# Keeping an intermediate weight combination in SBUF between the two products of a Winograd-Strassen unit that need it

## Chip, cores and metric

The kernel runs on one core of a Trainium2 chip. The metric is the device time in microseconds (us). The engines are TensorE (PE; PEld is its weight load), VectorE (DVE), ScalarE (ACT), GpSimd (POOL) and SyncE (SP), which issues the DMAs of this kernel. Each engine takes its instructions in the order in which they were written down for it, and waits on semaphores for what the others make.

## Reference

One decoder layer over 2048 positions of width 1024, in float32. An input projection is cut into two head groups, a gated MLP (A) and a Mamba-2 scan (B); their outputs are joined and projected back.

```python
h = rms_norm(x, pre_w)
proj = jnp.einsum('bld,dc->blc', h, w_in)
u, v, zg, z, xbc, dt_raw = jnp.split(proj, SPLITS, axis=-1)
y_a = spatial_gating(u, v, zg, v_norm_w, v_norm_b, ws, bs, gmlp_norm_w)
y_b = ssd_mixer(xbc, z, dt_raw, conv_w, conv_b, dt_bias, a_log, d_skip, ssd_norm_w)
mixed = jnp.einsum('blc,cd->bld', jnp.concatenate([y_a, y_b], axis=-1), w_out)
return x + rms_norm(mixed, post_w)
```

## The kernel before

The two projections are cut into seven **units**, numbered 0 to 6 (the list `UNITS`). Each unit multiplies a 2x2 arrangement of blocks of the activations (side A) with a 2x2 arrangement of blocks of the weights (side B), by the seven products P1 to P7 of the Winograd form of Strassen's scheme. Units 0 to 5 go through the sets (P1, P2), (P6, P7), (P4), (P5, P3); within a set through two block pairs p, the products, and two halves j. This makes 28 **steps** a unit, in each of which PE runs 24 matmuls of 128x512: every float32 operand is split into a high and a low part, and `mm3` (L165 to L167) forms three partial products. Unit 6 is the output projection, with four halves j and 56 steps.

Side B of a step is made by `make_b`, once for both pairs p. It loads blocks of 128x1024 (512 KB) into tiles "r" of `rpool` (7 buffers), combines them on DVE, and `split` writes the high part (ACT, L160) and the low part (DVE, L161) to a tile "b" of `bpool` (5 buffers). With q, t, r the blocks (0,1), (1,1), (0,0) of the weights, P6 forms T3 = t - q (L795) and **T2 = T3 + r** (L800). T2 is multiplied in P6, and is needed again in P4, whose operand is block (1,0) minus T2 (L819). P7 takes T3 from its tile; P5 subtracts two loaded blocks (L815). Between P6 and P4, T2 goes to DRAM and back: `store` puts the write on a list (L801), from which SP issues it some 5 us of the program's own count later (L230), and P4 loads it as a second tile "r" (L817, issued at L153). Side A of units 1 to 5 needs no arithmetic: it is loaded ready split, 1 MB a step (L736), into 3 buffers. In unit 0, S2, the like intermediate of side A, is already kept in SBUF by two POOL copies (L749) and two subtractions of halves (L773).

Beside the products run **tasks**: generators that are advanced between steps and put the scan of group B (lines 359 to 475) and the gating of group A (lines 553 to 627) between the matmuls. The names that matter here: `E` is a decay matrix, loaded from DRAM (L381), shifted (L389), passed through the exponential (L394) and masked (L431); `xdt` (L434) and E feed the matmuls `y_ps` (L448); `junk` (L184) is the output of a sum of squares, whose result goes through `s_ms`/`g_ms` (L171, DVE) and `s_r`/`g_r` (L173, POOL) to the scaling of `y` (L471, L627, both ACT). L598 and L613 on DVE and L615 on ACT belong to the gating.

`after` (L868) takes the accumulators `acc` away. P1 is copied out by ACT (L876), and P2 is then summed onto the same accumulator: its first matmul on each of the four accumulators waits for the copy of P1. `acc` has 5 banks of PSUM. SBUF tiles of 128x512 come from `gpool` (32 buffers), for the tasks, the stores and the copies of S2.

The order on each engine is set ahead of the run by the Tile scheduler, by its own reckoning of when data and buffers come free. A removed or added instruction can thus change the order of others.

Of the kernel before, what the change touches and what calls it, by code (L numbers as in the profile page):

```python
# [11 lines left out]
ALU = mybir.AluOpType  # L12
# [39 lines left out]
def hybrid_kernel(ctx: ExitStack, tc: tile.TileContext, x, x_t, pre_w, w_u, w_o, w_dt,  # L52
                  v_w, v_b, ws_t, bs_t, gn_w, conv_w, conv_b, dt_bias, a_log, d_skip, sn_w,
                  post_w, out):
    nc = tc.nc
# [15 lines left out]
    def gfull(name):  # L71
        return gpool.tile([P, 3 + T], F32, name=name, tag="g")

    def gt(name):
        return gfull(name)[:, 0:T]
# [4 lines left out]
    def rt(name):  # L80
        return rpool.tile([P, 2, T], F32, name=name, tag="r")
# [8 lines left out]
    t_d = {(u, j): dram.tile([P, 2, T], F32, name=f"t{u}{j}") for u in range(7) for j in range(2 if u < 6 else 4)}  # L90
# [58 lines left out]
    def load(pieces):  # L149
        res = []  # L150
        for src in pieces:
            t = rt("r")
            nc.sync.dma_start(out=t, in_=src)  # L153
            res.append(t)
        return res

    def split(pool, name, t):

        w = pool.tile([P, 2, 2, T], F32R, name=name)
        nc.scalar.activation(w[:, :, 0, :], t, AF.Copy)  # L160
        nc.vector.tensor_tensor(w[:, :, 1, :], t, w[:, :, 0, :], ALU.subtract)  # L161
        return w
# [61 lines left out]
    def store(dst, src, then=None):  # L224
        stores.append((now[0] + BEHIND, dst, src, then))
# [554 lines left out]
            store(a_d[p][name, j], w[:, :, :, :].bitcast(F32))  # L780
        yield w

    t3 = {}

    def make_b(u, name, j):
        piece = lambda k, n: w_u[u, k, n, j] if u < 6 else w_o[k, n, j]
        tt = nc.vector.tensor_tensor
        if name in PLAIN_B:
            t, = load([piece(*PLAIN_B[name])])
            yield  # L790
        elif name == "P6":
            if u < 6:
                q, t, r = load([piece(0, 1), piece(1, 1), piece(0, 0)])
                yield
                tt(t, t, q, ALU.subtract)  # L795
                t3[u, j] = t
            else:
                t, r = load([t3_d[j], piece(0, 0)])
                yield
            tt(r, t, r, ALU.add)  # L800
            store(t_d[u, j], r)  # L801
            t = r
        elif name == "P7":
            if u < 6:
                yield
                t = t3.pop((u, j))
            else:
                t, q = load([piece(1, 1), piece(0, 1)])
                yield
                tt(t, t, q, ALU.subtract)  # L810
                store(t3_d[j], t)
        elif name == "P5":
            t, q = load([piece(0, 1), piece(0, 0)])
            yield
            tt(t, t, q, ALU.subtract)  # L815
        else:
            t, q = load([piece(1, 0), t_d[u, j]])  # L817
            yield
            tt(t, t, q, ALU.subtract)  # L819
        yield split(bpool, "b", t)  # L820
# [12 lines left out]
    def look_ahead(i):  # L833
# [10 lines left out]
        def load_b(n, u, p, name, j):  # L844
            if p == 0:
                made_b[u, name, j] = make_b(u, name, j)
                next(made_b[u, name, j])
# [74 lines left out]
    for group in groups:  # L922
        i = group[0]
        u, p, name, j = steps[i][:4]
        _, channels, _, nj = UNITS[u]
# [81 lines left out]
```

## Time and profile before

| | |
|---|---|
| Runs | 1585.33, 1588.78, 1590.7 us; median 1588.78 us |
| Profiled execution | own time 1584.35 us, span 1582.6 us |
| Mean granted TensorE clock | 0.979 |
| Busy share | PE 95%, PEld 80%, DVE 68%, ACT 52%, POOL 25% |
| DMA | 494.63 MB, mean 313 GB/s |

The span runs from the first to the last instruction of the profiled execution; its own time holds 1.75 us more. A busy share is the part of the span in which an engine worked. A wait is idle time of an engine just before an instruction, put down to what ended it. Unit 1 begins at about 244 us, unit 2 at 439, unit 3 at 632, unit 4 at 829, unit 5 at 1032 and unit 6 at 1254 us.

### The profile page before, as it was taken

What the parts mean: (1) busy time and instruction counts of PE and PEld (TensorE: products, weight loads), DVE (VectorE), ACT (ScalarE), POOL (GpSimd) and SP (SyncE); (2) the same over time, 40 slices, a digit from 0 to 9 for tenths busy, and PEclk for the clock granted to TensorE, in tenths of its full rate; (3) what the DMA queues carried; (4) which work ended last, traced back from release to release, by engine and by line L of the source; (5) the groups of instructions that cost most, each with busy time, mean ns of one, the idle gap of its engine ahead of it and who ended that gap; (6) DMA issues with size and microseconds to landing.
All of it is one profiled execution on the core that took longest, in us unless ns stands there. A gap on an engine that the chain in (4) does not pass through costs nothing.

```text
span 1582.6 us, 21521 instructions
## 1 busy us (share of the span) xinstructions
PE 1508.9 (95%) x7268; PEld 1258.4 (80%) x7268; DVE 1068.9 (68%) x1708; ACT 819.8 (52%) x1769; POOL 390.1 (25%) x449
## 2 busy tenths in 40 slices
PE   4979999899999999999999999989999999999996
PEld 3868887788888888888778888867888878888775
DVE  3476874678665576567786768764665646587698
ACT  4432324655676545654466666859737742333332
POOL 1000000234232333342234515353523300000022
PEclk9988999999999999999999999989999999999999
DMA  9799999999998799986998788866776598897998
GB/s 333 264 371 357 338 411 397 392 340 366 374 349 311 240 353 341 329 316 238 333 338 319 271 299 275 279 229 225 276 252 242 193 302 326 275 384 239 341 351 333
DMA packets 160847, 494.63 MB, mean 313 GB/s; under 512 B 19040, under 2 KB 35808, under 8 KB 140768
## 3 DMA queue, kind: packets, MB, share of 16 engines
q1 hardware_dynamic: 160736, 493.25, 85.9%
q8 instruction: 57, 0.93, 0.2%
q14 instruction: 54, 0.44, 0.1%
HBM read 373.51 MB, written 119.67 MB: 312 GB/s over the span
## 4 chain that ended last, share of the span: by engine, by line
PE 57%; DMA 13%; DVE 11%; ACT 7%; issue 3%; POOL 1%; SPq 1%; DVEq 0%; ACTq 0%; POOLq 0%
PE acc L165 16%; PE acc L167 16%; PE acc L166 16%; DMA E<-scr 3%; DMA r<-yd 3%; PE y_ps L448 3%; ACT E L389 2%; DMA r<-w_o 2%; PE y_ps L451 1%; PE st_ps L453 1%; DVE cv_out L372 1%; DVE a L161 1%; PE s_ps L594 1%; PE y_tp L553 1%; DVE b L161 1%
## 5 line engine op out<-in xcount | busy, mean ns | idle before, releaser
L165 PE MATMUL acc<-b,a 128*128 128x512 f32 x1344 | 544.6, 406 | 16.1 <-DMA a<-as0P 5.4
L166 PE MATMUL acc<-b,a 128*128 128x512 f32 x1344 | 527.3, 392 | 0.0
L167 PE MATMUL acc<-b,a 128*128 128x512 f32 x1344 | 520.2, 393 | 4.3 <-DVE a L161 4.3
L165 PEld LDWEIGHTS acc<-b,a 128*128 128x128 f32 x1344 | 253.7, 189 | 71.3 <-DMA a<-as0P 5.6
L167 PEld LDWEIGHTS acc<-b,a 128*128 128x128 f32 x1344 | 253.2, 188 | 60.2 <-DVE a L161 6.3
L166 PEld LDWEIGHTS acc<-b,a 128*128 128x128 f32 x1344 | 254.0, 189 | 49.3
L160 ACT ACTIVATE a<-r 128x1024 fp32r<-128x1024 f32 x96 | 101.1, 1057 | 200.8 <-PE acc L167 88.5
L165 PE MATMUL acc<-a,b 128*128 128x512 f32 x448 | 182.4, 414 | 8.3 <-ACT b L160 4.2
L372 DVE SCALAR_TENSOR_TENSOR cv_out<-cv_raw,cw,cv_out 128x512 f32<-128x512 f32 x192 | 155.1, 810 | 41.5 <-ACT cv_out L370 39.5
L161 DVE TENSOR_TENSOR b<-r,b 128x1024 fp32r<-128x1024 f32 x112 | 141.9, 1270 | 60.6 <-ACT b L160 60.4
L166 PE MATMUL acc<-a,b 128*128 128x512 f32 x448 | 180.3, 403 | 0.8 <-DVE a L161 0.8
L167 PE MATMUL acc<-a,b 128*128 128x512 f32 x448 | 177.7, 400 | 0.0
L160 ACT ACTIVATE b<-r 128x1024 fp32r<-128x1024 f32 x112 | 117.2, 1052 | 86.9 <-PE acc L167 33.1
L161 DVE TENSOR_TENSOR a<-r,a 128x1024 fp32r<-128x1024 f32 x96 | 117.3, 1223 | 50.5 <-ACT a L160 50.3
L165 PEld LDWEIGHTS acc<-a,b 128*128 128x128 f32 x448 | 87.2, 195 | 27.4 <-ACT b L160 4.3
L184 ACT ACTIVATE junk<-y 128x128 bf16<-128x128 f32 (+1 forms) x192 | 65.5, 341 | 83.1 <-POOL y L465 71.4
L457 POOL TENSOR_TENSOR state<-state,ex 128x256 f32<-128x256 f32 x60 | 46.9, 781 | 239.5 <-PE y_ps L451 239.4
L166 PEld LDWEIGHTS acc<-a,b 128*128 128x128 f32 x448 | 86.8, 194 | 19.6 <-DVE a L161 1.8
L167 PEld LDWEIGHTS acc<-a,b 128*128 128x128 f32 x448 | 86.4, 193 | 18.9 <-issue 0.2
L436 POOL TENSOR_TENSOR xde<-xtok,dte 128x256 f32<-128x256 f32 x64 | 52.3, 824 | 165.0 <-ACT xtok L408 158.7
L173 POOL TENSOR_TENSOR o_r<-o_ms,mhalf 128x1 f32<-128x1 f32 x16 | 19.0, 1198 | 295.1 <-DVE o_ms L171 285.0
L389 ACT ACTIVATE E<-E,cs 128x128 f32<-128x128 f32 x256 | 79.6, 390 | 22.2 <-DMA E<-scr 22.2
(163 smaller groups left out, 2125.8 us busy)
## 6 DMA issues: line engine op xcount, KB each, us to landing
a<-as0P SPq DMA_DIRECT2D x64, 1024.0 KB, 7.4
a<-as1P SPq DMA_DIRECT2D x64, 1024.0 KB, 6.2
r<-w_u SPq DMA_DIRECT2D x108, 512.0 KB, 6.4
r<-yd SPq DMA_DIRECT2D x72, 512.0 KB, 5.3
r<-hd SPq DMA_DIRECT2D x48, 512.0 KB, 7.5
r<-w_o SPq DMA_DIRECT2D x36, 512.0 KB, 5.2
E<-scr SPq DMA_DIRECT2D x64, 256.0 KB, 7.4
yd<-yT SPq DMA_DIRECT2D x64, 256.0 KB, 4.4
```

Source lines behind the costliest of these rows:

```text
L160: nc.scalar.activation(w[:, :, 0, :], t, AF.Copy)
L161: nc.vector.tensor_tensor(w[:, :, 1, :], t, w[:, :, 0, :], ALU.subtract)
L165: nc.tensor.matmul(dst, lhsT=a_hi, rhs=b_hi, start=first, stop=False, skip_group_check=True)
L166: nc.tensor.matmul(dst, lhsT=a_hi, rhs=b_lo, start=False, stop=False, skip_group_check=True)
L167: return nc.tensor.matmul(dst, lhsT=a_lo, rhs=b_hi, start=False, stop=last, skip_group_check=True)
L173: nc.gpsimd.tensor_tensor(r, ms, mhalf[:, 0:n], ALU.pow)
L184: nc.scalar.activation(junk[:, 0:n], src, AF.Square, accum_out=dst)
L372: nc.vector.scalar_tensor_tensor(cv, raw[:, j:j + T], cw[:, ti, j:j + 1], cv, ALU.mult, ALU.add)
L389: nc.scalar.activation(E[:, h, :], E[:, h, :], AF.Relu, scale=-1.0, bias=dts[self.b]["cs"][:, o + h:o + h + 1])
L436: nc.gpsimd.tensor_tensor(h4(xde[:, :]), xc, hv(d["dte"], g, c), ALU.mult)
L448: nc.tensor.matmul(yps[:, h * HD:(h + 1) * HD], lhsT=E[:, h, :], rhs=xdt[:, h * HD:(h + 1) * HD], start=True, stop=True)
L457: nc.gpsimd.tensor_tensor(h4(st[:, :]), h4(st[:, :]), ev(d["ex"], 1, g, c), ALU.mult)
```

## The change

In units 1 to 5, T2 is no longer written to DRAM. Two POOL copies put its halves in two tiles `t2` of `gpool`, and P4 loads block (1,0) alone and subtracts the halves one by one on DVE. Units 0 and 6 stay as they were.

```diff
-    t3 = {}
+    t3, t2_in = {}, {}
...
             tt(r, t, r, ALU.add)
-            store(t_d[u, j], r)
+            if 0 < u < 6:
+                t2_in[u, j] = [gt("t2") for _ in range(2)]
+                for kk in range(2):
+                    nc.gpsimd.tensor_copy(t2_in[u, j][kk], r[:, kk, :])
+            else:
+                store(t_d[u, j], r)
             t = r
...
+        elif 0 < u < 6:
+            t, = load([piece(1, 0)])
+            yield
+            for kk, t2 in enumerate(t2_in.pop((u, j))):
+                tt(t[:, kk, :], t[:, kk, :], t2, ALU.subtract)
         else:
             t, q = load([piece(1, 0), t_d[u, j]])
```

Lines behind the change move: L876 is L886 in the changed kernel, L901 is L911, the copies stand at L804, the subtraction of P5 at L820 and that of the halves at L825.

**ACT, unit 4, second pair, around P1.** Before, from the gating's `sg` up to the scaling by `g_r`. In these rows `p1` is the copy of P1.

```order
L394 ACT_TABLE_LOAD
...
L160 ACTIVATE b_7770<-r_7692 128x2x512 [waits PE_49]
...
L876 ACTIVATE p1_7700<-acc_7618 128x512 [waits DMAHW7_49,PE_49]
L876 ACTIVATE p1_7708<-acc_7633 128x512 [waits PE_49]
...
L184 ACTIVATE junk_253,g_ss_7533<-y_7503 128x128 [waits Activation_49,Pool_49]
L876 ACTIVATE p1_7723<-acc_7640 128x512 [waits PE_49]
...
L184 ACTIVATE junk_253,g_ss_7533<-y_7503 128x128 [waits Activation_49]
L471 ACTIVATE y_7314<-y_7314,s_r_7604 128x256 [waits Pool_49]
...
L876 ACTIVATE p1_7754<-acc_7662 128x512 [waits PE_49]
...
L627 ACTIVATE y_7455<-y_7455,g_r_7671 128x128 [waits Pool_49]
```

The same stretch of the changed kernel; the four loads of ACT's tables ahead of it are the first rows.

```order
L394 ACT_TABLE_LOAD
...
L615 ACT_TABLE_LOAD
...
L394 ACT_TABLE_LOAD
...
L615 ACT_TABLE_LOAD
...
L184 ACTIVATE junk_253,g_ss_7545<-y_7515 128x128 [waits Activation_49,Pool_49]
...
L471 ACTIVATE y_7326<-y_7326,s_r_7616 128x256 [waits Pool_49]
...
L408 ACTIVATE xtok_7672<-xt_tp_7667 128x512 [waits DMAHW0_49,PE_49]
L886 ACTIVATE p1_7716<-acc_7630 128x512
L627 ACTIVATE y_7467<-y_7467,g_r_7683 128x128 [waits Pool_49]
...
L160 ACTIVATE b_7789<-r_7708 128x2x512 [waits PE_49]
L886 ACTIVATE p1_7724<-acc_7645 128x512 [waits PE_49]
...
L886 ACTIVATE p1_7739<-acc_7652 128x512 [waits DMAHW0_49,PE_49]
```

The scalings by `s_r` and `g_r` (L471, L627), which wait for POOL, now stand ahead of copies of P1 that they stood behind. From the first E of this stretch (E_7659, E_7647 before) to the first copy of P1 the whole order has six ACT_TABLE_LOAD rows where it had three, because the E work (L389, L394) and the gating's `sg` (L615) are laced differently.

**DVE, unit 5, first pair.** Before, the two subtractions of T2 for P4 (L819), the low parts behind them, and P5's subtraction (L815), between pieces of the gating and the scan.

```order
L819 TENSOR_TENSOR r_10495<-r_10495,r_10497 128x1024 [waits DMAHW7_49,DMAHW6_49]
...
L901 TENSOR_TENSOR u2_8272<-u2_8272,acc_9208 128x512 [waits PE_49]
L161 TENSOR_TENSOR b_9606<-r_9504,b_9606 128x2x512 [waits Activation_49]
...
L819 TENSOR_TENSOR r_10561<-r_10561,r_10563 128x1024 [waits DMAHW2_49,DMAHW1_49]
L161 TENSOR_TENSOR b_9977<-r_9915,b_9977 128x2x512 [waits Activation_49]
L434 TENSOR_TENSOR xdt_9282<-xtok_8983,dt1_577 128x256 [waits PE_49]
L460 TENSOR_TENSOR y_9297<-y_ps_9287,xtok_8983 128x256 [waits PE_49]
L463 TENSOR_TENSOR yo_9299<-y_ps_9287,ex1_1125 128x256 [waits PE_49]
L815 TENSOR_TENSOR r_10757<-r_10757,r_10759 128x1024 [waits DMAHW5_49,DMAHW4_49,DVE_49]
L598 TENSOR_TENSOR y_9400<-s_ps_9395,SB_252 128x256 [waits PE_49,Pool_49]
```

The same two places of the changed kernel.

```order
L911 TENSOR_TENSOR u2_8287<-u2_8287,acc_9224 128x512 [waits PE_49]
L161 TENSOR_TENSOR b_9622<-r_9520,b_9622 128x2x512 [waits Activation_49]
L911 TENSOR_TENSOR u2_8302<-u2_8302,acc_9246 128x512 [waits PE_49]
...
L911 TENSOR_TENSOR u2_8342<-u2_8342,acc_9290 128x512 [waits PE_49]
L161 TENSOR_TENSOR b_9997<-r_9931,b_9997 128x2x512 [waits Activation_49]
L434 TENSOR_TENSOR xdt_9298<-xtok_8999,dt1_577 128x256 [waits PE_49]
L460 TENSOR_TENSOR y_9313<-y_ps_9303,xtok_8999 128x256 [waits PE_49]
L463 TENSOR_TENSOR yo_9315<-y_ps_9303,ex1_1125 128x256 [waits PE_49]
L598 TENSOR_TENSOR y_9416<-s_ps_9411,SB_252 128x256 [waits PE_49,Pool_49]
```

L819 and L815 have left this stretch; the subtractions of halves (L825) and of P5 (L820) stand 60 to 80 rows further back, between `cv_out` (L372) and `xdt` (L434) rows of the second pair.

**SP, unit 1, ahead of the side A load of the first step of P6.** Before; `t10` is the write of T2, `as1P20` and `as1P21` are writes of side A, `as0P60` is the load.

```order
L230 DMA as1P20_116<-a_2166 128x2048 [waits DMAHW6_49,DVE_49]
...
L230 DMA t10_150<-r_2175 128x1024 [waits DMAHW0_49,DVE_49]
L398 DMA zs_2359<-zs0_164 128x256 [waits DMAHW1_49]
L398 DMA zs_2389<-zs0_164 128x256 [waits DMAHW2_49]
L153 DMA r_2628<-w_u 128x1024 [waits DMAHW3_49]
L230 DMA as1P21_117<-a_2219 128x2048 [waits DMAHW4_49,DVE_49]
L736 DMA a_2282<-as0P60_104 128x2048 [waits DMAHW5_49,PE_49]
```

The changed kernel.

```order
L230 DMA as1P20_116<-a_2166 128x2048 [waits DMAHW4_49,DVE_49]
L398 DMA zs_2395<-zs0_164 128x256 [waits DMAHW5_49]
L153 DMA r_2634<-w_u 128x1024 [waits DMAHW6_49]
L381 DMA E_2261<-scr0_939 128x512 [waits DMAHW7_49]
...
L153 DMA r_2700<-hd2_2_94 128x1024 [waits DMAHW3_49,DVE_49,Pool_49]
L230 DMA as1P21_117<-a_2219 128x2048 [waits DMAHW4_49,DVE_49]
L153 DMA r_2702<-w_u 128x1024 [waits DMAHW5_49]
L736 DMA a_2285<-as0P60_104 128x2048 [waits DMAHW6_49,PE_49]
```

The write of T2 has left, the four loads of E (three of them ahead of as1P20 before) have moved down, and two loads of 512 KB for later steps (r_2700 is a block of side A, r_2702 one of weights) stand ahead of the load as0P60, which they stood behind. In both kernels the loads of E stand ahead of it.

## Rows read from the trace of the kernel before

**Rows 1.** The page: span, then busy time and share of two engines, instructions.

```profile
span 1582.6 us, 21521 instructions
...
PE 1508.9 (95%) x7268; PEld 1258.4 (80%) x7268; DVE 1068.9 (68%) x1708; ACT 819.8 (52%) x1769; POOL 390.1 (25%) x449
```

**Rows 2.** Waits, whole span: who waited for whom: total us, times, longest.

```profile
PE acc L165 <- DMA a<-as0P: 5.4, 2, 5.2
...
DVE r L819 <- DMA r<-t: 3.0, 2, 2.2
```

**Rows 3.** DMA issues by line, KB of one, median us from issue to landing.

```profile
E<-scr SPq DMA_DIRECT2D x64, 256.0 KB, 7.4
...
t<-r SPq DMA_DIRECT2D x20, 512.0 KB, 6.7
r<-t SPq DMA_DIRECT2D x20, 512.0 KB, 6.0
```

**Rows 4.** Single lines: duration in ns (min/median/max), first and last start.

```profile
L749 POOL COPY s<-r x8: 609/615/1071, 114.2 to 158.2; 128x512 f32<-128x512 f32 x8
...
L773 DVE TENSOR_TENSOR r<-r,s x8: 682/684/686, 200.4 to 227.6; 128x512 f32<-128x512 f32 x8
...
L161 DVE TENSOR_TENSOR b<-r,b x112: 1205/1219/1765, 38.2 to 1532.6; 128x1024 fp32r<-128x1024 f32 x112
```

**Rows 5.** Timeline of DVE, unit 5: start, us, instruction, idle before it and releaser.

```profile
1028.12 1.22 DVE L819 TENSOR_TENSOR r<-r 128x1024 f32<-128x1024 f32 x1 [0.83 <-DMA r<-t]
...
1037.82 1.22 DVE L819 TENSOR_TENSOR r<-r 128x1024 f32<-128x1024 f32 x1 [2.17 <-DMA r<-t]
...
1045.44 1.22 DVE L815 TENSOR_TENSOR r<-r 128x1024 f32<-128x1024 f32 x1 [4.26 <-DMA r<-w_u]
```

**Rows 6.** Timeline of PE, unit 5, the same columns.

```profile
1047.94 0.63 PE L553 MATMUL y_tp<-ident,y 128*128 128x128 f32 x4 [1.67 <-DVE y L598]
...
1061.02 1.97 PE L448 MATMUL y_ps<-xdt,E 128*128 128x64 f32 x8 [4.32 <-DVE xdt L434]
```

**Rows 7.** The chain that ended last, unit 5: start, us, what.

```profile
1049.37 1.66 POOL g_r L173
...
1060.63 0.35 DVE xdt L434
```

**Rows 8.** Windows: length, busy us of PE, PEld, DVE, ACT, POOL; PEclk; DMA; GB/s.

```profile
840.00:850.00 10.00, 10.00 (x58) 8.70 (x57) 7.06 (x14) 3.50 (x10) 7.30 (x9) 1.00 1.01 399
...
1050.00:1053.00 3.00, 2.79 (x16) 2.39 (x14) 1.83 (x5) 1.96 (x7) 2.46 (x3) 0.58 0.98 378
...
1062.00:1065.00 3.00, 2.81 (x9) 1.90 (x8) 1.62 (x4) 1.23 (x5) 0.61 (x1) 0.50 0.22 81
```

**Rows 9.** Timeline of ACT, unit 4.

```profile
853.19 0.63 ACT L376 ACTIVATE cv_out<-cv_out 128x512 f32<-128x512 f32 x1 [2.40 <-DVE cv_out L372]
...
866.42 1.28 ACT L394 ACT_TABLE_LOAD   x1
...
871.12 1.07 ACT L876 ACTIVATE p<-acc 128x512 f32<-128x512 f32 x2
...
874.09 1.72 ACT L471 ACTIVATE y<-y,s_r 128x256 f32<-128x256 f32 x4
...
877.11 2.46 ACT L627 ACTIVATE y<-y,g_r 128x128 f32<-128x128 f32 x8
```

**Rows 10.** Timeline of SP, unit 4.

```profile
842.47 0.32 SPq L736 DMA_DIRECT2D a<-as1P  x1
...
851.89 1.59 SPq L381 DMA_DIRECT2D E<-scr  x3
```

**Rows 11.** Timeline of PE, unit 4: first matmul of P2 on its first two accumulators.

```profile
871.76 0.50 PE L165 MATMUL acc<-b,a 128*128 128x512 f32 x1
...
873.24 0.39 PE L165 MATMUL acc<-b,a 128*128 128x512 f32 x1
```

**Rows 12.** Timeline of PE, unit 1.

```profile
300.56 0.80 PE L165 MATMUL acc<-b,a 128*128 128x512 f32 x1 [5.19 <-DMA a<-as0P]
```

## The prediction

> **What bounds the kernel now.** I read the page first: PE works 1508.9 us of the 1582.6 us span [rows 1], so the time is PE's own work plus the places where PE stands still. The list of waits, read next, shows what of this the T2 round trip could own. DVE waits for a T2 reload (r<-t) only 3.0 us in all, twice [rows 2], although twenty tiles come back that way with a median of 6.0 us each [rows 3]. So eighteen of the twenty reloads (ten of which the change removes, with ten of the twenty writes) are early enough to cost nothing. The timeline of DVE puts both waits in unit 5: 0.83 us at 1028.12 and 2.17 us at 1037.82. A third follows at 1045.44, 4.26 us for the weights of P5, whose load could start only when a buffer of the "r" pool came free behind the second subtraction [rows 5]. The chain that ended last runs through all three, then through g_r and xdt [rows 7], and PE pays at its end: 1.67 us before y_tp and 4.32 us before y_ps [rows 6]. Behind these its clock is granted at 0.58 and 0.50 of full speed, the latter the 1.2 GHz level [rows 8]. The reader should see that only one unit of the five waits for T2.
>
> The other places to look at are those where the change moves instructions next to a PE wait or makes one: side A's load in unit 1, for which PE waits 5.19 of that line's 5.4 us [rows 12, 2], and the copies of P1 in unit 4.
>
> **The change, part by part, in us on the own time of 1584.35.**
>
> *Operations.* Ten DVE subtractions of 1.22 us [rows 5] become twenty of 0.684, by the like halves of side A [rows 4]: 13.7 for 12.2 us, 0.15 more per tile, hidden where DVE idles (68% busy, rows 1). Twenty POOL copies of 0.615 us [rows 4] add 12.3 us to an engine that is 25% busy. Ten writes and ten reloads of 512 KB go, 10.5 of 494.63 MB. I cost all this at 0 by itself. If DVE's cover is gone the price is 0.15 a tile, 1.5 in all.
>
> *Unit 5, the waits for T2.* DVE's three waits, 0.83 + 2.17 + 4.26 = 7.26 us, leave this stretch with their instructions, as the two DVE pieces show. Not all of that reaches PE. The xdt behind the second subtraction can run some 3 us earlier, and g_r, held by the third wait, up to 4.8 earlier, so the xdt of 1060.63 [rows 7] may come at about 1055.7. PE wanted it at 1061.02 - 4.32 = 1056.7, but will itself be 1.67 us (y_tp) and about 1.9 us (less half speed) earlier: at 1053.1. A wait of 2.6 in place of 4.32 remains. Saved are 3.6 + 1.7 and some of the half speed behind: I take **-6.5**. Bounds: all of it, 1.67 + 4.32 of idle and about 5 us of half speed (0.42 of 3 us by the first window and half of some 8 us by the second, rows 8), gives -11; if g_r is held by the scan's work instead, only y_tp's wait goes, -2.
>
> *Unit 5, where the halves go.* They and P5's subtractions now stand near 1098 to 1113, where DVE is nearly full: 4 x 0.684 + 1.22 = 4 us more there, while the copies of P1 stand ahead of some squares that they stood behind. Bounds -2.5 to +4; I take **0**.
>
> *Unit 4, the order on ACT.* Here the change costs something that its diff doesn't show. The four E loads, of which three were issued at 851.89, now go out right behind the load of 842.47 [rows 10]. E's shift and exponential on ACT move forward and are laced with the gating: six table loads where three stood, 1.28 us each [rows 9]. The scalings by s_r (four, 1.72 us) and g_r (eight, 2.46 us) now stand ahead of copies of P1 that stood ahead of them [rows 9]. PE has nothing in hand there: P2's first matmul starts at 871.76 [rows 11], right at the end of the first copy of P1 (871.12 + 0.6, half of the row for two). In the profile ACT works without a gap from 853.19 to that point, 18.5 us [rows 9]. The new order puts 3 x 1.28 + 1.72 = 5.6 us more ahead of the copy, so 24.1 us. It may begin when E is there: 842.9 + 7.4 (median, rows 3) = 850.3, or up to 3.8 us sooner, since about 1.5 MB less is queued ahead at 399 GB/s [rows 8]. I take 849. Then the first copy ends at 873.1, about 873.5 with a short wait for s_r, and the second, behind g_r's scalings (2.46), a split (1.1) and itself (0.6), at 877.5. PE wants that one at 873.24 [rows 11]: **4.2 late**, 1.7 to 5.5 by the two times of E. Behind g_ms, DVE now has to wait for the POOL copies, which stand behind g_r, then do four halves and a further P5 subtraction, 4 us, ahead of the xdt that PE needs next: 0 to 3 beyond PE's own delay, I take 1.4. Half speed behind such idle time: 0 to 2.5, I take 0.9. Together **+6.5**, from +1.7 to +11.
>
> *Unit 1.* Ahead of the side A load that PE waits for at 300.56 [rows 12], T2's write (0.5 MB) leaves and two loads (1 MB) come in. 0.5 MB at 399 GB/s, the rate in unit 4, is **+1.3**. Bounds: -5.2 (the whole wait) to +3 (both loads and half speed). Units 2 and 3: no wait of PE stands near T2; 0, within 1 either way.
>
> *A rule weighed.* POOL's copies are at best 609 ns, at most 1071, and DVE's low parts (two inputs from SBUF) 1205 to 1765 [rows 4]: each is now and then longer by about 0.5 us. The Trainium skill, page "SBUF — State Buffer", section "SBUF: two separate sides", says that a GpSimd instruction and a VectorE one with two SBUF inputs share a port pair that one of them holds for its whole length. The spread agrees in kind, but no row shows which held which. By the rule every copy would hold DVE up for its 0.615 us, 12.3 in all; by the rows at most 0.55 us (1765 - 1219) each.
>
> **Sum.** -6.5 + 0 + 6.5 + 1.3 = +1.3: 1585.65 own time. The profiled execution is 4.43 us under the median of the runs, so on the median's basis 1590.1; I say **1590**. A difference of 0.3% (4.8 us) is about what a measurement of this kernel can tell from no change.
>
> **Rivals.**
> 1. *Unit 5's gain comes whole and ACT's order costs little* (-11 + 2 + 1 = -8, so 1581). For it: the chain through r<-t [rows 7], and ACT has idle time of 2.40 us before 853.19 [rows 9] into which E's work can move. Against: P1's copies stand behind two POOL results.
> 2. *Slower: P2 of unit 4 waits for ACT.* Place: the second copy of P1, behind g_r's scalings. Price: 5.5 + 3 + 2.5 = +11, with a gain in unit 5 of only 4: +8, so 1597. It decides from a second copy about 7 us late, that is, when the E tiles land after 850 and PE falls to half speed. Against: fewer DMAs are queued there.
> 3. *The copies and the two-input subtractions hold each other*: at 0.55 us each, four copies in unit 4 and four in unit 5 cost 4.4 where DVE is full, 1594.5. For it: the spread of [rows 4]. Against: half of the copies meet an idle DVE. The rule of the Trainium skill named above would lead here.
> 4. *The change hides its own saving*: the round trip was hidden but for unit 5, and the buffer that T2 holds until its copy delays P5's weights there as the reload did. 0, so 1588.8.
>
> **How the numbers follow.** Forecast and rival 4, near no change: 0.42. Rival 1 and parts of it, with unit 5's gain larger than unit 4's loss: 0.28. Rivals 2 and 3: 0.30, of which 3 has 0.05. The range of 8 in 10 reaches past both ends, 1578 to 1601; the likeliest case by itself has 1585 to 1595.
>
> **What would show each step.** Right: no L819 left in units 1 to 5 and none of the three DVE waits near 1028 to 1045; PE's waits before y_tp and y_ps in that place under 3 us together; in unit 4 a PE wait on ACT's copy of P1 (acc L165, released by p) of some 4 us near 873 to 878; 44 ACT_TABLE_LOAD rows in the order of the changed kernel for 40; in unit 1 the wait for as0P still there, about 1 us longer. Wrong would be: no PE wait in unit 4, because E landed before 847 or the scalings didn't have to wait; the y_ps wait of 4.32 unchanged, with another releaser; or a new stretch at half speed in a unit that I cost at 0.

## The result: 0.9% slower, and the profile after

The changed kernel takes 1602.41 us (median of 5 runs, 1598.21 to 1604.64), the kernel before 1588.10 us in the same comparison (5 runs, 1583.73 to 1590.70). The ratio is 1.0088, 95% interval 1.0064 to 1.0112: slower by some 14 us, between 10 and 18. The prediction was 1590 us with a range of 1578 to 1601. It forecast no change; the result is a loss, just outside the range. The profiled execution of the changed kernel took 1602.41 us, its span is 1600.6 us. One execution of run 8 below took 3876 us where its other eleven took 1582 to 1593; it counts in none of that run's numbers.

The page of the changed kernel, as [rows 1]: the span grew by 18.0 us, PE's busy time by 4.6 of these; it counts a matmul of 128x512 with 0.63 us at the lower clock and 0.39 at the higher.

```profile
span 1600.6 us, 21501 instructions
...
PE 1513.5 (95%) x7268; PEld 1259.1 (79%) x7268; DVE 1075.0 (67%) x1718; ACT 826.7 (52%) x1773; POOL 401.1 (25%) x469
```

The list of PE's waits over the whole span (who waited for whom, total us, times, longest). The line for the load as0P answers to [rows 2]; `sg` is new, and the wait for xdt that was to shrink is still there with 4.1 us.

```profile
PE acc L165 <- DMA a<-as0P: 7.4, 2, 6.2
...
PE y_ps L448 <- DVE xdt L434: 5.3, 2, 4.1
PE acc L165 <- ACT sg L615: 5.2, 3, 3.8
```

The DMA issues, as [rows 3]: ten writes and ten reloads of T2 are left where twenty of each stood, so the change does what it says.

```profile
t<-r SPq DMA_DIRECT2D x10, 512.0 KB, 6.2
r<-t SPq DMA_DIRECT2D x10, 512.0 KB, 5.6
```

The new lines by themselves, as [rows 4]: copies and halved subtractions cost per piece what the prediction took from the like lines of side A.

```profile
L804 POOL COPY t<-r x20: 605/614/1079, 283.3 to 1111.5; 128x512 f32<-128x512 f32 x20
...
L825 DVE TENSOR_TENSOR r<-r,t x20: 673/688/1208, 295.4 to 1119.5; 128x512 f32<-128x512 f32 x20
```

**Where the time went.** From the timeline of PE I took each unit's length, from its first product matmul to that of the next unit. One profiled execution a kernel; us:

| kernel | unit 1 | unit 2 | unit 3 | unit 4 | unit 5 |
|---|---|---|---|---|---|
| before | 194.8 | 192.8 | 196.6 | 203.2 | 222.1 |
| the change | 197.0 | 192.8 | 197.2 | **213.6** | 220.3 |

Unit 4 owns 10.4 us. Unit 1 owns 2.2, and unit 5 gives back 1.8. Unit 6, which the change doesn't touch, is 5.3 us longer in this profile (333.8 for 328.5); over the twelve kernels below it lies between 327.8 and 334.1 without regard to the change, so I leave it out as scatter. Unit 4 begins at 833.0 us now (828.8 before), unit 5 at 1046.6 (1032.0).

PE's waits in units 1, 4 and 5 of the changed kernel (start, us, instruction, idle before it and releaser) answer to [rows 6, 11, 12]:

```profile
303.98 0.80 PE L165 MATMUL acc<-b,a 128*128 128x512 f32 x1 [6.19 <-DMA a<-as0P]
...
840.52 0.50 PE L165 MATMUL acc<-b,a 128*128 128x512 f32 x1 [1.19 <-DMA a<-as0P]
870.87 0.80 PE L165 MATMUL acc<-b,a 128*128 128x512 f32 x1 [3.77 <-ACT sg L615]
874.50 0.50 PE L165 MATMUL acc<-b,a 128*128 128x512 f32 x1 [0.71 <-ACT sg L615]
885.79 0.50 PE L165 MATMUL acc<-b,a 128*128 128x512 f32 x1 [0.36 <-ACT p L886]
...
902.53 1.11 PE L448 MATMUL y_ps<-xdt,E 128*128 128x64 f32 x8 [1.19 <-DVE xdt L434]
...
1072.17 1.97 PE L448 MATMUL y_ps<-xdt,E 128*128 128x64 f32 x8 [4.06 <-DVE xdt L434]
```

In unit 4 PE stood still 7.2 us in these five places, where the kernel before has none of these waits. The largest is for `sg`: this activation reads an accumulator straight out of PSUM (`sg<-acc`), so the bank isn't free for P1 of the second pair until it has run. Why it was late is seen on SP (first fence) and ACT (second), to be set beside [rows 10] and [rows 9]:

```profile
848.08 0.32 SPq L736 DMA_DIRECT2D a<-as1P  x1
848.45 1.98 SPq L381 DMA_DIRECT2D E<-scr  x4
```

```profile
855.98 2.45 ACT L389 ACTIVATE E<-E,cs 128x128 f32<-128x128 f32 x8 [1.76 <-DMA E<-scr]
858.45 1.28 ACT L394 ACT_TABLE_LOAD   x1
...
869.13 1.28 ACT L615 ACT_TABLE_LOAD   x1
870.43 0.38 ACT L615 ACTIVATE sg<-acc 128x256 f32<-128x256 f32 x1
870.83 1.28 ACT L394 ACT_TABLE_LOAD   x1
872.12 0.63 ACT L394 ACTIVATE E<-E 128x512 f32<-128x512 f32 x1
872.77 1.28 ACT L615 ACT_TABLE_LOAD   x1
874.06 0.66 ACT L615 ACTIVATE sg<-acc 128x256 f32<-128x256 f32 x2
...
879.30 1.71 ACT L471 ACTIVATE y<-y,s_r 128x256 f32<-128x256 f32 x4 [0.40 <-POOL s_r L173]
...
881.40 0.57 ACT L886 ACTIVATE p<-acc 128x512 f32<-128x512 f32 x1
881.87 2.44 ACT L627 ACTIVATE y<-y,g_r 128x128 f32<-128x128 f32 x8
...
885.17 0.57 ACT L886 ACTIVATE p<-acc 128x512 f32<-128x512 f32 x1
...
1061.29 2.45 ACT L627 ACTIVATE y<-y,g_r 128x128 f32<-128x128 f32 x8 [1.96 <-POOL g_r L173]
```

The loads of E stand behind the load as1P in SP's queue. That one left at 848.08, E at 848.45, and E was usable at 855.98. ACT stood idle for it (1.76 us), because all of E's shifts were queued ahead of the first `sg`. From there ACT has no gap until 878.9, with six table loads of 1.28 us. Four of these stand ahead of the first `sg`, which runs at 870.43. PE wanted its bank 3.77 us sooner.

Counted by steps (from the unit's start to the first matmul of a step, against the kernel before), the change is 1.3 us behind at the second step of unit 4, 1.5 at the fifth, 7.7 at the sixth, 8.5 at the ninth and 10.2 at the eleventh; after that it loses next to nothing. So `sg`, with the slow clock behind it, took 6.2 us, the load as0P 1.3, the stretch of P1's copies 0.8 and the stretch up to xdt 1.7.

On DVE in the same stretch the halves of T2 waited for POOL's copies, and P5's subtraction, which stands ahead of the xdt that PE waits for at 902.53, for its weights:

```profile
881.47 2.08 DVE L825 TENSOR_TENSOR r<-r,t 128x512 f32<-128x512 f32 x2 [2.36 <-POOL t L804]
...
897.64 1.23 DVE L820 TENSOR_TENSOR r<-r 128x1024 f32<-128x1024 f32 x1 [1.72 <-DMA r<-w_u]
```

The windows (columns as in [rows 8]) show PE's clock behind the waits: 0.64 of full speed right behind the wait for `sg`, where PE had done almost nothing for 4.1 us, and in unit 5 0.64 and then 0.50, the 1.2 GHz level, behind the wait for xdt, as before.

```profile
866.70:870.80 4.10, 0.39 (x2) 0.00 (x0) 0.00 (x0) 4.07 (x8) 0.00 (x0) 0.95 0.43 180
870.80:875.00 4.20, 3.43 (x8) 2.30 (x9) 0.00 (x0) 4.14 (x8) 1.89 (x3) 0.64 0.00 0
1071.00:1074.00 3.00, 1.83 (x9) 1.83 (x9) 2.53 (x5) 2.78 (x11) 0.83 (x2) 0.64 0.32 105
1074.00:1077.00 3.00, 2.41 (x7) 1.51 (x7) 1.18 (x3) 0.20 (x1) 1.05 (x2) 0.50 0.00 0
```

In unit 5 DVE's three waits of [rows 5] are gone, and PE's wait of 1.67 us before y_tp [rows 6] with them. DVE ahead of the xdt that PE waits for, with POOL's g_r in the second fence, to set beside [rows 7]:

```profile
1065.05 2.43 DVE L372 SCALAR_TENSOR_TENSOR cv_out<-cv_raw,cw,cv_out 128x512 f32<-128x512 f32 x3 [0.59 <-ACT cv_out L370]
...
1067.74 2.03 DVE L372 SCALAR_TENSOR_TENSOR cv_out<-cv_raw,cw,cv_out 128x512 f32<-128x512 f32 x2
1069.69 2.09 DVE L584 SCALAR_TENSOR_TENSOR v<-v,v_mv,row_w 128x256 f32<-128x256 f32 x3
1071.70 0.41 DVE L434 TENSOR_TENSOR xdt<-xtok,dt 128x256 f32<-128x256 f32 x1
```

```profile
1059.61 1.65 POOL L173 TENSOR_TENSOR g_r<-g_ms,mhalf 128x8 f32<-128x8 f32 x1 [0.32 <-DVE g_ms L171]
```

Measured from the unit's start, g_r begins at 13.0 us (17.4 before: 1049.37 - 1032.0), so it did come 4.4 us sooner. But ahead of xdt DVE still has five `cv_out` and three `v`, 6.6 us of work, and it begins with them only when ACT has delivered, behind the scaling by g_r (last row of the ACT fence above). xdt came 3.5 us sooner after the unit's start (25.1 for 28.6), and PE asked for it 3.2 us sooner (21.5 for 24.7): the wait stayed nearly as it was. By the same count of steps the change is 4.5 us ahead at the fourth step of unit 5, behind this stall, but only 1.8 from the eighth on.

### The profile page after: what moved, and what is told of

Its sections match the earlier page's. It is cut to its first block, busy times and chain, and to the rows that moved or that the text cites. A ratio compares the mean times of both kernels' runs of the same rounds, so it can differ in the third digit from the quotient of the medians.

```text
span 1600.6 us, 21501 instructions
## 1 busy us (share of the span) xinstructions
PE 1513.5 (95%) x7268; PEld 1259.1 (79%) x7268; DVE 1075.0 (67%) x1718; ACT 826.7 (52%) x1773; POOL 401.1 (25%) x469
## 4 chain that ended last, share of the span: by engine, by line
PE 53%; DMA 14%; DVE 11%; ACT 9%; issue 4%; POOL 1%; SPq 1%; DVEq 0%; ACTq 0%; POOLq 0%
PE acc L165 15%; PE acc L167 15%; PE acc L166 15%; DMA r<-yd 3%; DMA E<-scr 3%; PE y_ps L448 2%; ACT E L389 2%; DMA r<-w_o 2%; DVE b L161 1%; DMA r<-w_u 1%; PE y_ps L451 1%; PE st_ps L453 1%; DVE cv_out L372 1%; DMA a<-as0P 1%; DVE a L161 1%
## 5 line engine op out<-in xcount | busy, mean ns | idle before, releaser
L372 DVE SCALAR_TENSOR_TENSOR cv_out<-cv_raw,cw,cv_out 128x512 f32<-128x512 f32 x192 | 158.6, 831 | 36.3 <-ACT cv_out L370 34.5
L160 ACT ACTIVATE b<-r 128x1024 fp32r<-128x1024 f32 x112 | 117.3, 1052 | 89.6 <-PE acc L167 28.6
L389 ACT ACTIVATE E<-E,cs 128x128 f32<-128x128 f32 x256 | 79.7, 390 | 23.7 <-DMA E<-scr 23.5
L376 ACT ACTIVATE cv_out<-cv_out 128x512 f32<-128x512 f32 x64 | 40.2, 629 | 85.0 <-DVE cv_out L372 84.7
```

The lines of the kernel that those rows point to most:

```text
L372: nc.vector.scalar_tensor_tensor(cv, raw[:, j:j + T], cw[:, ti, j:j + 1], cv, ALU.mult, ALU.add)
L376: nc.scalar.activation(self.cv[i], self.cv[i], AF.Silu)
L389: nc.scalar.activation(E[:, h, :], E[:, h, :], AF.Relu, scale=-1.0, bias=dts[self.b]["cs"][:, o + h:o + h + 1])
```

## The experiments

The expectations of runs 1 to 8 and 10 go by letters. Theory A: unit 4 loses by ACT's order, E laced with the gating. Theory B: POOL's copies and the halved subtractions cost something in every unit. Theory C: the wait for xdt that is left in unit 5 is an effect of DVE's order. Theory D: it belongs to the chain of the gating behind g_r, and an edit of the order changes only its name. Each kernel was timed against the kernel before on the same chip. The times given are medians; the ratio is not their quotient and differs from it by up to 0.12% (run 10: 0.9996 beside 1587.17/1585.97 = 1.0008), so small differences are read from its interval alone. Beside the ratio the length of the unit in question is given, from its profile.

**1. u4_as_before.** The change in units 1, 2, 3 and 5.

```diff
-            if 0 < u < 6:
+            if u in (1, 2, 3, 5):
...
-        elif 0 < u < 6:
+        elif u in (1, 2, 3, 5):
```

> T2 stays in SBUF in units 1, 2, 3 and 5; unit 4 writes and reloads it as before, and ACT's order around P1 of unit 4 is again that of before. Theory A (the cost is ACT's order in unit 4: E's work laced with the gating, P1's copies behind the scalings): unit 4 falls from 213.6 us to about 203, the time to about 1592, ratio to before 1.000 to 1.005. Theory B (the POOL copies and the halved subtractions cost about the same in each unit that has them): four fifths of the 14.3 us stay, ratio about 1.007.

Measured: 1589.84 us for 1587.49, ratio 1.0024 (1.0006 to 1.0042). Unit 4 took 203.9 us, and PE has no listed wait in its first third. Most of the loss is unit 4's, but not all of it.

**2. u4_no_t2_at_all.** The kernel before, with T2 neither written nor reloaded nor subtracted in unit 4 (the subtraction of T2 from P4's operand is left out there), and no copies.

```diff
-            store(t_d[u, j], r)
+            if u != 4:
+                store(t_d[u, j], r)
...
+        elif u == 4:
+            t, = load([piece(1, 0)])
+            yield
```

> The kernel before, with T2 of unit 4 neither written, nor reloaded, nor copied, nor subtracted (P4 of unit 4 multiplies block (1,0) alone). Less work on every engine than before, but the scheduler again puts E's work ahead on ACT and the copies of P1 behind the scalings. A: slower than before by 6 to 11 us, unit 4 at 209 to 214 us, with PE waiting for sg or for P1's copies. B: nothing was added, so the same as before or up to 1 us faster, unit 4 at about 203.

Measured: 1595.45 us for 1587.49, ratio 1.0052 (1.0032 to 1.0071), unit 4 at 212.8 us. It has no POOL copy, no halved subtraction and no held tile, only less work than before, and it loses nearly what the change loses in unit 4. The list of PE's waits in that stretch names the same releaser:

```profile
PE acc L165 <- ACT sg L615: 4.1, 3, 1.5
```

So taking T2's round trip out is enough for the loss; what is put in its place is not needed for it.

**3. sbuf_and_traffic.** The change, with T2 written to DRAM and loaded back as well; the loaded tile isn't used.

```diff
             if 0 < u < 6:
...
+                store(t_d[u, j], r)
...
-            t, = load([piece(1, 0)])
+            t, _ = load([piece(1, 0), t_d[u, j]])
```

> The changed kernel with the write to DRAM and the reload of T2 put back beside the copies (the reloaded tile isn't used). All POOL copies and halved subtractions are there, and the DMA traffic of before; with it ACT's order in unit 4 changes once more: P1's copies stand ahead of the scalings and the gating's sg is spread. A: unit 4 at 203 to 207, time 1588 to 1595. B: at least as slow as the changed kernel, 1602 or more.

Measured: 1591.51 us for 1587.49, ratio 1.0032 (1.0019 to 1.0045), unit 4 at 208.3 us, just above what A expected. With more work than the change it is faster than the change. Its ACT rows in unit 4 still have five table loads between E and `sg`, but the first two `sg` stand ahead of every exponential and table load, and PE doesn't wait for `sg`:

```profile
856.60 0.38 ACT L615 ACTIVATE sg<-acc 128x256 f32<-128x256 f32 x1 [0.77 <-DVE y L613]
...
859.52 0.36 ACT L615 ACTIVATE sg<-acc 128x256 f32<-128x256 f32 x1
```

The unit is still 4.4 us over the 203.9 of run 1. PE waits there for another activation that stands behind the table loads, `xtok`, in two places, 1.8 and 1.3 us:

```profile
PE cb_ps L422 <- ACT xtok L408: 1.8, 1, 1.8
```

**4. copies_on_dve.** The copies of T2 on DVE.

```diff
-                    nc.gpsimd.tensor_copy(t2_in[u, j][kk], r[:, kk, :])
+                    nc.vector.tensor_copy(t2_in[u, j][kk], r[:, kk, :])
```

> The changed kernel with the copies of T2 on DVE in place of POOL. ACT's order in unit 4 is that of the changed kernel, letter by letter. A: no better than the changed kernel, 1600 to 1605, unit 4 at 211 to 216. B (POOL copies: late behind g_r, or sharing a port with DVE): most of the 14 us comes back, 1590 to 1595.

Measured: 1598.59 us for 1587.49, ratio 1.0075 (1.0056 to 1.0095), unit 4 at 211.7 us. The copies are shorter there, by the line's own durations:

```profile
L804 DVE COPY t<-r x20: 414/424/961, 283.6 to 1112.0; 128x512 f32<-128x512 f32 x20
```

The interval overlaps that of the change (1.0064 to 1.0112): no gain that can be told from POOL having no copies. It isn't a clean test of rival 3 (copies and two-input subtractions hold each other), as DVE now has twenty copies more, 8.5 us in all, which could hide a gain. The trace of the change answers that rival better. Six of POOL's twenty copies took 1.07 to 1.08 us in place of 0.61, and just these six began while DVE was in an operation with two inputs from SBUF; the other fourteen took at most 0.62. In the other direction, nine of the twenty halved subtractions took 1.06 to 1.21 us in place of 0.69, each of them beside a POOL operation. So the two do hold each other. In unit 4 the four copies (merged into one line; 0.61, 0.61, 1.07 and 1.07 us) stand beside the two halves that were shown at 881.47:

```profile
880.83 3.19 POOL L804 COPY t<-r 128x512 f32<-128x512 f32 x4
```

By the rule of the Trainium skill, page "SBUF — State Buffer", section "SBUF: two separate sides", one of the two holds their common port pair for its whole length. At its full price, an estimate, that is 4 x 0.615 = 2.5 us in unit 4. The trace agrees with the rule, at a lower price, since not every copy met such an operation: DVE's two halves took 2.15 us in place of 1.38, 0.8 more. Nor is it what costs unit 4 its 10 us: run 5 has two copies of 1.07 us and two halves of 1.07 and 1.10 there as well, and its unit 4 takes 205.2 us.

**5. e_behind_sg.** The change, with E's shifts and exponentials of unit 4 queued on ACT behind the last `sg`.

```diff
...
+            with tc.issue_after(sg_last[0]) if (self.b, self.g) == (3, 2) and sg_last else nullcontext():
+                for h in range(HG):
+                    nc.scalar.activation(E[:, h, :], E[:, h, :], AF.Relu, scale=-1.0,
...
+            with tc.issue_after(sg_last[0]) if (self.b, self.g) == (3, 2) and sg_last else nullcontext():
+                for c in range(NT):
+                    nc.scalar.activation(self.E[c], self.E[c], AF.Exp, scale=-1.0)
...
-        nc.scalar.activation(sg, t[:, GC:2 * GC], AF.Silu)
+        sg_last[:] = [nc.scalar.activation(sg, t[:, GC:2 * GC], AF.Silu).ins]
```

> The whole change, and one thing more: in unit 4 the shifts and exponentials of E of one group (L389, L394) are queued on ACT behind the gating's last sg. All copies, halved subtractions and DMAs stay as in the changed kernel; the order has 40 table loads again and P1's copies ahead of the scalings. A (order on ACT alone): unit 4 at 203 to 206 us, no PE wait on sg, time 1587 to 1592. B2 (in unit 4 it is the POOL copies behind g_r or the halves on DVE, and the order only goes with them): unit 4 stays above 209, time 1597 or more.

Measured: 1592.86 us for 1586.93, ratio 1.0046 (1.0029 to 1.0063), unit 4 at 205.2 us for 213.6. T2 stays in SBUF and POOL copies it; the edit is to ACT's order alone. The scheduler moved some forty of DVE's 270 rows in unit 4 with it, and a few on POOL and SP. In the place of six table loads there is one, ahead of the first exponential:

```profile
869.72 3.61 ACT L391 ACTIVATE E<-E,cs 128x128 f32<-128x128 f32 x12
873.35 1.28 ACT L397 ACT_TABLE_LOAD   x1
```

The wait for `sg` is gone from the list, and what is left in that stretch is the wait that the prediction had named, for P1's copy:

```profile
PE acc L165 <- ACT p L889: 1.4, 1, 1.4
```

With run 2 and the rows of the changed kernel this shows the cause of unit 4's loss: with ACT's order mended and all of the change's own work kept, 8.4 us of the 10.4 come back. What DVE's shifted rows add to that wasn't tested by itself. The Trainium skill, page "ScalarE: Activation LUTs", section "Table sets: the hidden batching unit", advises to batch activations by table set, which is what this order does; the trace agrees, with one load in place of six and the shorter unit. But run 3 shows that the number of loads isn't all: five of them behind the first two `sg` cost PE no wait for `sg`, only the shorter ones for `xtok`.

**6. only_unit_5.** The change in unit 5 alone (`u == 5` in both conditions).

> The change in unit 5 alone. A and C: units 1 and 4 as before, unit 5 at 218 to 219 (before: 222), so 3 to 4 us faster than before, 1583.5 to 1585, ratio 0.9975. Rival (unit 5's gain is given back by the copies and halves at 1098 to 1113): unit 5 at 221 or more, no difference.

Measured: 1583.51 us for 1586.93, ratio 0.9984 (0.9968 to 1.0001), unit 5 at 217.5 us. The fastest kernel of the study, at the edge of what can be told from before. The wait that was to shrink is whole:

```profile
1060.27 1.10 PE L448 MATMUL y_ps<-xdt,E 128*128 128x64 f32 x8 [4.17 <-DVE xdt L434]
```

**7. e_behind_sg_xdt_first**, **8. before_xdt_first.** In unit 5 the next chunk's xdt stands ahead of `cv_out` and `v` on DVE: in run 7 with run 5's edit, in run 8 in the kernel before.

```diff
...
+                early = (cur.b, cur.g) == (1, 3) and c + 1 < NT
+                if early:
+                    cur.operands(c + 1)
...
-                    nxt.conv(c)
+                    with tc.issue_after(xdt_last[0]) if early else nullcontext():
+                        nxt.conv(c)
...
-                if c + 1 < NT:
+                if c + 1 < NT and not early:
```

> As the kernel before this one in the list, and in unit 5 the last xdt of one chunk group is queued on DVE ahead of the next group's cv_out and v rows instead of behind them. C (what is left of unit 5's stall, 4.1 to 4.4 us before y_ps in every kernel whose unit 5 has no T2 reload, is DVE's order): that wait falls under 1 us, unit 5 from about 218 to 212 to 214, time 4 to 6 us under e_behind_sg. D (the wait belongs to the gating's chain and only changes its name): unit 5 stays at 217 or more.

> The kernel before with nothing of the change, but with the same xdt of unit 5 queued ahead of cv_out and v on DVE. C: y_ps's wait of 4.32 us goes although T2 still makes its round trip, 3 to 6 us faster, 1582 to 1585. If instead the reload chain through r<-t owns that wait, as the chain view of before reads: no difference, 1586 to 1589.

Measured: run 7 1587.82 us for 1586.93, ratio 1.0014 (0.9999 to 1.0029), unit 5 at 215.6; run 8 1589.29 for 1586.93, ratio 1.0021 (1.0007 to 1.0035), unit 5 at 221.4. In both the wait for xdt is replaced by one for `state`, which stands behind the same block on DVE. Run 7:

```profile
1065.26 1.11 PE L561 MATMUL y_tp<-ident,y 128*128 128x128 f32 x4 [3.94 <-DVE state L462]
```

Run 8, with a wait for side A later on:

```profile
1059.13 1.11 PE L558 MATMUL y_tp<-ident,y 128*128 128x128 f32 x4 [3.53 <-DVE state L459]
...
1093.66 0.79 PE L165 MATMUL acc<-b,a 128*128 128x512 f32 x1 [4.15 <-DMA a<-as0P]
```

PE waits for DVE's block of `cv_out` and `v`, not for one operation in it. But the order does gain time at the stall: run 8 is 4.1 us ahead of the kernel before at the fourth step of unit 5, and 33 to 36 us after the unit's start it has 0.92 of full speed where before has 0.50. It loses 3.4 of these again by the eleventh, at the new wait for side A. Run 7 has no such wait: its unit 5 is 5.0 us shorter than run 5's (215.6 for 220.6), and the whole kernel too (1587.82 for 1592.86), as C expected of the time. Run 10 was made to see whether that holds without the rest of the change.

**9. only_unit_1** (`u == 1` in both conditions).

> Only unit 1 keeps T2 in SBUF; units 2 to 5 are as before. Theory U (unit 1 pays for the change by itself, as the kernels with it there averaged 197.9 us for unit 1 against 195.3 us without): unit 1 of about 198 us, the kernel some 2.5 us slower than before, near 1590, ratio 1.0015. Theory W (those 2.5 us come only with the change in the units next to it): unit 1 stays at 195 us and the ratio at 1.000.

Measured: 1589.05 us for 1585.97, ratio 1.0008 (0.9993 to 1.0023), unit 1 at 197.7 us. The unit grew as the first theory said, with a longer wait for the load as0P than before's 5.19 us; the ratio can't tell 2.5 us from none.

```profile
302.10 0.79 PE L165 MATMUL acc<-b,a 128*128 128x512 f32 x1 [6.93 <-DMA a<-as0P]
```

**10. only_unit_5_xdt_first.** Run 6 with the edit of run 8.

> T2 stays in SBUF in unit 5 alone, and xdt of the next chunk stands ahead of cv_out and v on DVE there. Theory D with what e_behind_sg_xdt_first showed (the wait changes its name, but unit 5 took 215.6 us where 220 stood): unit 5 at 214 to 216 us, the kernel 6 to 7 us under before, near 1581, ratio 0.996. If the reordering gives nothing without the change in the other units: as only_unit_5, unit 5 at 217.5 and ratio 0.998.

Measured: 1587.17 us for 1585.97, ratio 0.9996 (0.9983 to 1.0009), unit 5 at 218.7 us. The 6 to 7 us that I expected from run 7 didn't come. As in run 8, a wait for side A stands behind the stall, and so it does in run 12 (3.60 us); only run 7 is without it:

```profile
1092.86 0.50 PE L165 MATMUL acc<-b,a 128*128 128x512 f32 x1 [3.69 <-DMA a<-as0P]
```

So xdt ahead of the block moves PE's time to the next load of side A in three kernels of four. Why not in run 7 is open.

**11. e_behind_sg_not_unit_1**, **12. all_mended_not_unit_1.** Runs 5 and 7 with unit 1 as before (`1 < u < 6`).

> The kernel of e_behind_sg (the change, with unit 4's shifts and exponentials of E queued on ACT behind the last sg) with unit 1 as before, so T2 stays in SBUF in units 2 to 5. Theory U: unit 1 at 195 to 196 us where e_behind_sg had 199.7, the kernel 2.5 to 4 us under it, 1589 to 1590, ratio about 1.0015 to 1.003. Theory W: no more than 1 us under e_behind_sg, ratio about 1.004.

> T2 stays in SBUF in units 2 to 5; unit 4's shifts and exponentials of E stand behind the last sg on ACT, and unit 5's xdt ahead of cv_out and v on DVE. Theory U: e_behind_sg_xdt_first less the 2.5 us of unit 1, ratio about 0.9995. Theory W: as e_behind_sg_xdt_first, 1.0014. Should it still stand over only_unit_5_xdt_first by 3 us or more, units 3 and 4 have a cost that ACT's order in unit 4 doesn't tell.

Measured: run 11 1588.42 us for 1585.97, ratio 1.0016 (0.9996 to 1.0035); run 12 1591.71 for 1585.97, ratio 1.0031 (1.0016 to 1.0045). Unit 1 fell to 195.2 and 195.9 us, but unit 2 rose to 198.8 and 198.5, where it takes 192.7 to 195.8 in the kernels that keep T2 in units 1 and 2. PE's waits in unit 2 of run 11 tell of three new small stalls, where run 5 has 1.2 and 0.4 us:

```profile
PE cb_ps L425 <- ACT xtok L411: 2.3, 1, 2.3
PE acc L165 <- DVE u L903: 1.7, 2, 1.2
PE acc L165 <- ACT p L889: 1.6, 1, 1.6
```

In these two kernels, leaving unit 1 out moves its price to unit 2. One of the two ratios fell against its twin (1.0046 to 1.0016), the other rose (1.0014 to 1.0031): no gain that holds. Run 12 stands 4.5 us over run 10 (1591.71 for 1587.17), past the 3 us that its expectation had set for a cost outside ACT's order in unit 4; by the two profiles most of it is unit 2 (198.5 for 192.4).

## Why the prediction was wrong

Over the fourteen profiles (before, the change and the twelve runs), the units with T2 in SBUF can be set against the same units without. Unit 1: 197.9 us on average in seven kernels, 195.3 in seven, with no overlap (196.6 is the least with, 195.9 the most without). Unit 2: 193.5 for 192.9 where unit 1 has the change too. Unit 3: 198.2 for 196.5, with overlap. Unit 4: 213.6 for 204.0 (six kernels, 203.2 to 204.5). Unit 5, with xdt in its old place: 218.9 in seven kernels for 222.8 in three. The sum, 2.5 + 0.6 + 1.8 + 9.6 - 3.9 = +10.6 us, stands against 14 measured with an interval of 10 to 18. The prediction's sum for the same terms was +1.3. The 10.6 lies inside the interval; what is missing to 14 isn't assigned.

- **Unit 4, +6.5 for 9.6 to 10.4.** The cause was named rightly: ACT's order, E laced with the gating, six table loads. The step that failed is the wait that it was to make: "the second, behind g_r's scalings", P1's copy, "4.2 late". That wait was 0.36 us. PE paid ahead of it, at a term that the sum hadn't got: `sg` holds the banks that P1 itself is to be written to, and the waits for it, 3.77 + 0.71 us with 0.64 of full clock, took 6.2 us by the count of steps. Once PE was late, P1's copies cost it little, although the first came 48.4 us after the unit's start for 42.3 before. The time of E was wrong too: I took it as usable at 849, 20.2 us after the unit's start, and it came at 23.0. Half of the difference is the load of side A that E stands behind in the queue, which left 1.4 us later after the unit's start than before; the other half is E's own way, 7.5 us from issue to ACT for the 6.1 that I had taken. At nothing stood also the load as0P, 1.19 us at 840.52. The wait for xdt has the size that I worked out (1.19 for 1.4), but that is partly luck: DVE did wait for POOL's copies, 2.36 us, but the wait that ends last ahead of that xdt is the one for P5's weights (1.72 at 897.64). That the sum of +6.5 comes near the loss measured is in part luck as well: its largest term didn't occur.
- **Unit 5's gain was mis-sized, -6.5 for -3.9.** The step that failed is "so the xdt of 1060.63 may come at about 1055.7". I let xdt follow g_r's gain of up to 4.8 us and the second subtraction's 3. g_r gained 4.4, but xdt stands behind DVE's block of `cv_out` and `v`, which waits for ACT behind g_r's scalings, so xdt gained 3.5, and PE's demand for it 3.2. The wait is 4.06 us for the 2.6 forecast, and the half speed behind it stayed. At the stall the change gains 4.5 us of the 6.5. The stretch behind it, in which the halves go and which I put at 0, loses 2.7 of them again in the change; the one new wait in that stretch is 0.70 us for `sg`. The halves alone don't make it: run 1 has them there too and gives back 0.3. What does is open. Runs 7, 8 and 10 show DVE's block as what holds PE at the stall.
- **Unit 1, +1.3 for +2.5.** The wait for the load as0P grew by 1.0 us in the profile shown (5.19 to 6.19) and to 6.93 in run 9, the size of my estimate. Run 3 has T2's write back in the queue and no such loads ahead; it waits 5.56 us there, but 1.45 for a later load as0P, and its unit 1 takes 197.2 us as well. So the exchange ahead of that one load isn't the whole price; what the rest is stays open.
- **Units 2 and 3, 0 for +0.6 and +1.8.** The ranges of unit 3 just touch (197.2 to 200.4 us with, 195.4 to 197.4 without), so some of its part may be real; what makes it is open. The place of the cost in unit 2 depends on unit 1 (runs 11 and 12). I had reasoned that no wait of PE stands near T2 there; the new waits of run 11 are for xtok, `u` and P1's copy, other work whose order moved.
- **Operations at 0** held as far as can be told: run 2, without any, is within 0.8 us of the change in unit 4, and run 3, with all of them and the DMAs too, is shorter there. What the prediction left open, which operation held which, the trace does show (run 4); it costs DVE 0.8 us in unit 4.

Of the rivals the second was nearest: slower, by ACT's order in unit 4, from the point at which E lands after 850 and PE falls to half speed. Both came about (E at 855.98, which is 851.8 by the unit's start of before). Its price of 11 in unit 4 is near the 9.6 to 10.4 measured; its place, the second copy of P1, was not, and unit 1's and unit 3's costs came on top. The signs that I had named split accordingly: the waits of DVE for T2 are gone, ACT has 44 table loads for 40, the wait for as0P is 1 us longer, but the stall at P1's copy is 0.36 us and the one before y_ps nearly unchanged, with the same releaser.

## What to carry to other kernels

Where a scheduler sets the order on each engine, taking two DMAs out of a unit is an edit of every queue: run 2, with less work and nothing added, lost nearly as much in unit 4 as the change did. So read the order of the changed kernel for every instruction that frees a PSUM bank or a buffer for PE, not only those next to the edit, and follow a moved load back to what stands ahead of it in its queue. Here the removal of transfers that nobody waited for gained nothing; only unit 5's was waited for, and the versions that touch unit 5 alone are the only ones whose ratio isn't above 1, though neither can be told from 1.

## What the runs showed of the hardware

- A table load on ACT took 1.28 us in every row, and the activations around it follow within 0.02 us: the exponential at 872.12 ends at 872.75, the load starts at 872.77, and `sg` at 874.06. The Trainium skill, page "ScalarE: Activation LUTs", section "What ACT_TABLE_LOAD costs", states 1283 ns for the load, as here, and a drain of some 1380 ns beside it for each switch. No such drain is seen in these rows; the measurement decides, 1.28 us a switch.
- The same copy of 128x512 float32 took 614 ns on POOL and 424 on DVE (medians of twenty), and the shorter one didn't make the kernel measurably faster.
- Where a POOL copy and a DVE operation with two SBUF inputs met, the later one took longer: in the changed kernel six copies of 0.61 us took 1.07, and nine halved subtractions of 0.69, beside POOL copies and products, took 1.06 to 1.21. Not every pair does this: two halves beside g_r, a POOL operation of 128x8, kept their 0.68 and 0.69 us, and a DVE sum with one operand in PSUM (0.69 us at 153.29) and the copy beside it (0.62) kept theirs.
